# Six plain blocks instead of four at the head of each FFN, in a fused transformer block

## The chip, the cores and the metric

One core of a Trainium2 chip runs the whole kernel. The time is the device time of one execution in microseconds (us). An execution also leaves a profile; its span is the time from the first to the last instruction. TensorE (PE) multiplies, ScalarE (ACT), VectorE (DVE) and GpSimd (POOL) do elementwise work, SyncE (SP) issues nearly all DMAs. Each engine works through its own queue in order.

## The reference

One layer for 512 tokens of width 1024, in fp32: a half-weighted SwiGLU FFN, a mixer with two kinds of attention, and another half-weighted FFN, then a norm.

```
x = x + 0.5 * swiglu(rmsnorm(x, norm_ffn1), w_ffn1_gate, w_ffn1_up, w_ffn1_down)
x = x + hybrid_mixer(rmsnorm(x, norm_mix), w_in, ..., w_out, rel_bias)
x = x + 0.5 * swiglu(rmsnorm(x, norm_ffn2), w_ffn2_gate, w_ffn2_up, w_ffn2_down)
return rmsnorm(x, norm_final)

swiglu(h, w_gate, w_up, w_down) = (silu(h @ w_gate) * (h @ w_up)) @ w_down     # d_ff = 2816
```

The mixer projects x to queries, keys and values of 16 heads of 64. Eight heads do block attention (MoBA; at this length every earlier block of 256 tokens is selected, so it is causal attention with a relative bias), eight do NSA: a compressed branch, a selected branch (all blocks at this length) and a window branch, each weighted by a gate.

## The kernel before

x is held transposed, as eight tiles `xs[k]` of 128 features x 512 tokens. Every fp32 operand of a matmul is split into a high and a low half (`halves`, `split`: ScalarE makes the high half, VectorE the low one, L80/L81 and L196/L197), and a product is three matmuls (`mm3`, L86 to L88): a *triple*. The norm's gain goes into x before the product (`gained`, L122/L123, the 16 `xo` tiles in `ffn.xg`), its per-token root R (a row of 512, `rows_of_roots`) after it.

An FFN has 22 blocks `f` of 128 of d_ff. Its work is a list of `Step`s that `go` puts on TensorE in just that order; loads, sums and splits are given out 26, 12.8 and 8.6 us of step cost ahead. The order on the other engines, and when a buffer is given, is decided by a planner at build time, which simulates the program with its own costs, takes instructions in program order as far as they are ready, and lets a later one go first where an earlier one is not ready or has no buffer.

- `plain(fs)`: blocks without tricks, two halves of the depth (j) and gate and up (m): per block four steps of 12 matmuls of 512 columns. It needs only the gained x. At its end, `finish` scales by R (L260), applies silu, multiplies (L262), and `kept` stores the result `h` as two halves (L224, L225).
- `pair(f)`: two blocks with seven products where plain blocks need eight (Strassen's scheme in Winograd's form): 14 steps of 12 matmuls of 256 columns. It needs sums of weights (L288), weight splits into `sph` and `spl` (three buffers each), and sums and blocks of the normed x: `sums_of_x(k)` (L186 to L190) and `blocks_of_x(k)`, for k from 0 to 3. The first product stays in its bank while a copy `wc` is taken from it (L304).
- `down`: h times the down weights, 8 output tiles times one triple per block; a weight chunk serves eight triples. A finished output tile is added to x (L465).
- `mixed` lays the down triples of the group before between the steps of the pairs of a group.

The FFNs begin with four plain blocks, so that TensorE has work while R and the sums of x are made. Then come 24 (`LEAD`) of the 32 down triples of these blocks unmixed, the other eight beside the next two pairs, and so on in groups of four; the last group has two blocks. FFN1 ends with 16 unmixed triples, FFN2 with 16 in which the roles are turned, so that the result comes out by tokens. `h` tiles come from a pool of 16, which in FFN1 holds seven tiles of the bias tables too. In FFN1 the sums of squares are made from `xs` (`squares`: ScalarE squares, VectorE adds at L138, TensorE sums over partitions at L144).

In the mixer, heads are done in three chunks each of logits, turn and values, with the projections, and later the output product `w_out`, as filler between them: a generator gives out filler units of one depth tile, and `target(i)` says how many of them shall have been given by chunk i (1.4 a chunk in NSA, 0.6 in block attention). `need` forces what a head needs.

```
        def target(i):
            if i < n_nsa:
                return 1.4 * i
            return 1.4 * n_nsa + 0.6 * (i - n_nsa)
```

## Time and profile before

| | |
|---|---|
| time, three runs | median 1039.27 us (1038.64 to 1039.96) |
| the profiled execution | 1037.35 us, span 1035.6 us |
| PE busy | 991.0 us (96%), 6096 matmuls |
| DVE, ACT, POOL busy | 759.1 us (73%), 526.2 us (51%), 138.8 us (13%) |
| mean granted TensorE clock | 0.987 |
| DMA | 104.45 MB, 101 GB/s over the span |

FFN1 reaches from the start to about 370 us, the mixer from there to 672, FFN2 to the end. A page of the profile has the span in 40 slices of 25.9 us; a digit is the busy share of a slice in tenths. A row of the list in order of time reads: start, duration, engine, line, operation, output <- inputs, form, and in brackets how long the engine sat idle before it and who ended that. Matmuls overlap in their pipeline, so the pace is read from their starts and not from their durations.

### The profile page before, as it was taken

To read this page: it belongs to the slowest core of one execution; us is meant where nothing else is said; L and a number is where in the kernel's file an instruction comes from. 1 tells how busy PE (TensorE), PEld (TensorE's weight loads), DVE (VectorE), ACT (ScalarE), POOL (GpSimd) and SP (SyncE) were. 2 spreads that over 40 slices of the span, in tenths; PEclk is the share of its full clock that TensorE was granted. 3 is DMA by queue.
4 is the path that set the end of the run, shared out by engine and by line. 5 is a ranking of instruction groups with operands and counts; after the bars stand their busy time and mean duration, and the time that the engine had idled before them with its cause. 6 is when DMAs were issued, how large, how long until landed. Compare 5 with 4: busy or idle time off the path is not lost.

```text
span 1035.6 us, 15887 instructions
## 1 busy us (share of the span) xinstructions
PE 991.0 (96%) x6096; PEld 868.3 (84%) x6096; DVE 759.1 (73%) x1232; ACT 526.2 (51%) x897; POOL 138.8 (13%) x169
## 2 busy tenths in 40 slices
PE   8979999999999999999999998997999999999996
PEld 6858898999999887787787786686899999999985
DVE  6985758877766486778778966779577776677745
ACT  6633443444443264658667856655244443344326
POOL 0000000000000040046553562500000000000002
PEclk9989999999999999999999999999999999999999
DMA  9323463323321125541011141363333333332102
GB/s 314 120 82 122 123 182 106 122 82 104 121 82 33 52 75 154 177 127 57 30 48 31 52 122 42 102 223 87 97 99 106 97 108 102 123 119 65 62 1 82
DMA packets 40688, 104.45 MB, mean 101 GB/s; under 512 B 9089, under 2 KB 13906, under 8 KB 40612
## 3 DMA queue, kind: packets, MB, share of 16 engines
q1 hardware_dynamic: 40324, 103.29, 32.0%
q8 instruction: 48, 0.79, 0.3%
q14 instruction: 28, 0.23, 0.1%
q10 hardware_dynamic: 288, 0.14, 0.1%
HBM read 97.98 MB, written 5.30 MB: 100 GB/s over the span
## 4 chain that ended last, share of the span: by engine, by line
PE 52%; DVE 5%; ACT 3%; issue 2%; DMA 1%; ACTq 0%; DVEq 0%; SPq 0%
PE pd L87 4%; PE pd L86 4%; PE pd L88 4%; PE pu L86 3%; PE pu L88 3%; PE pu L87 3%; PE pw L87 3%; PE pw L88 3%; PE pw L86 3%; PE pp L88 3%; PE pp L86 3%; PE pp L87 3%; PE ps_t L895 2%; PE pgu L86 1%; PE pgu L87 1%
## 5 line engine op out<-in xcount | busy, mean ns | idle before, releaser
L196 ACT ACTIVATE sph<-aw 128x1024 fp32r<-128x1024 f32 x126 | 133.7, 1061 | 247.7 <-PE pu L87 110.0
L197 DVE TENSOR_TENSOR spl<-aw,sph 128x1024 fp32r<-128x1024 f32 x126 | 153.7, 1221 | 30.6 <-ACT sph L196 30.4
L80 ACT ACTIVATE whi<-raw 128x1024 fp32r<-128x1024 f32 (+3 forms) x109 | 105.7, 971 | 109.3 <-PE pd L87 41.5
L87 PE MATMUL pd<-h,whi 128*128 128x512 f32 x336 | 134.8, 401 | 10.9 <-DVE h L225 10.9
L86 PE MATMUL pd<-h,whi 128*128 128x512 f32 x336 | 134.7, 401 | 3.8 <-DVE x L465 1.8
L88 PE MATMUL pd<-h,wlo 128*128 128x512 f32 x336 | 132.8, 395 | 0.0
L86 PE MATMUL pu<-th,sph 128*128 128x256 f32 x432 | 120.6, 279 | 4.1 <-ACT wc L304 3.3
L88 PE MATMUL pu<-th,spl 128*128 128x256 f32 x432 | 120.1, 278 | 0.0
L87 PE MATMUL pu<-tl,sph 128*128 128x256 f32 x432 | 120.0, 278 | 0.0
L288 DVE TENSOR_TENSOR aw<-aw 128x1024 f32<-128x1024 f32 x72 | 87.8, 1220 | 37.9 <-DMA aw<-in_wgu 37.7
L81 DVE TENSOR_TENSOR wlo<-raw,whi 128x1024 fp32r<-128x1024 f32 (+3 forms) x83 | 100.0, 1207 | 20.0 <-ACT whi L80 19.2
L465 DVE SCALAR_TENSOR_TENSOR x<-pd,x 128x512 f32<-128x512 f32 x88 | 60.3, 688 | 59.1 <-PE pd L88 59.1
L86 PEld LDWEIGHTS pu<-th,sph 128*128 128x128 f32 x432 | 81.1, 188 | 10.1 <-ACT wc L304 5.0
L87 PEld LDWEIGHTS pu<-tl,sph 128*128 128x128 f32 x432 | 81.6, 189 | 3.6
L88 PEld LDWEIGHTS pu<-th,spl 128*128 128x128 f32 x432 | 81.1, 188 | 0.0
L88 PE MATMUL pw<-xo,spl 128*128 128x256 f32 x288 | 79.9, 277 | 0.0
L86 PE MATMUL pw<-xo,sph 128*128 128x256 f32 x288 | 79.9, 277 | 0.0
L87 PE MATMUL pw<-xo,sph 128*128 128x256 f32 x288 | 79.8, 277 | 0.0
L87 PEld LDWEIGHTS pd<-h,whi 128*128 128x128 f32 x336 | 64.3, 191 | 18.3 <-DVE h L225 12.6
L88 PEld LDWEIGHTS pd<-h,wlo 128*128 128x128 f32 x336 | 64.3, 191 | 14.2
L86 PEld LDWEIGHTS pd<-h,whi 128*128 128x128 f32 x336 | 63.9, 190 | 13.5 <-DVE x L465 4.0
L87 PEld LDWEIGHTS pw<-xo,sph 128*128 128x128 f32 x288 | 54.3, 189 | 2.7
(250 smaller groups left out, 2452.9 us busy)
## 6 DMA issues: line engine op xcount, KB each, us to landing
aw<-in_wgu SPq DMA_DIRECT2D x72, 512.0 KB, 4.2
raw<-in_wd1a SPq DMA_DIRECT2D x20, 512.0 KB, 3.5
raw<-in_wd2a SPq DMA_DIRECT2D x20, 512.0 KB, 3.7
raw<-in_w_a SPq DMA_DIRECT2D x16, 512.0 KB, 3.6
raw<-in_wgu SPq DMA_DIRECT2D x15, 512.0 KB, 6.9
raw<-in_w SPq DMA_DIRECT2D x8, 512.0 KB, 5.1
raw<-in_w_o SPq DMA_DIRECT2D x16, 256.0 KB, 3.2
scr_t<-scr_r SPq DMA_DIRECT2D x8, 384.0 KB, 8.6
```

Source lines behind the costliest of these rows:

```text
L80: nc.scalar.activation(hi[:, s], src[:, s], AF.Copy)
L81: (nc.gpsimd if side[0] else nc.vector).tensor_tensor(lo[:, s], src[:, s], f32(hi[:, s]), ALU.subtract)
L86: nc.tensor.matmul(p, w[0], v[0], start=first, stop=False, skip_group_check=again)
L87: nc.tensor.matmul(p, w[0], v[1], start=False, stop=False, skip_group_check=again)
L88: nc.tensor.matmul(p, w[1], v[0], start=False, stop=last, skip_group_check=again)
L196: nc.scalar.activation(hi, v, AF.Copy)
L197: nc.vector.tensor_tensor(lo, v, f32(hi), ALU.subtract)
L288: nc.vector.tensor_tensor(to, x, y, op)
L465: nc.vector.scalar_tensor_tensor(xs[d], p, 0.5, xs[d], ALU.mult, ALU.add)
L895: nc.tensor.transpose(p[:, wide:wide + 128], lps[qi][:, j * 128:(j + 1) * 128], ident)
```

## The change

1. `PLAIN = 6`: both FFNs begin with six plain blocks, in two groups of three (in each group first all j = 0, then all j = 1); 16 blocks are left for eight pairs in four groups of four, and no group of two. Of the 48 triples of the six blocks 12 (`LEAD`) stand unmixed, 36 beside the next two pairs. `sums_of_x` is posted at steps 4, 6, 8, 10 and `blocks_of_x` at 4, 18, 18, 23 (before: sums from step 5 (FFN1) or 4 on, at 0, 1, 3 and 5 steps' distance, blocks at the first, 8, 10, 15). The last group has four blocks: 32 unmixed triples at the end of each FFN.
2. In FFN1 the squares are taken from four token-major tiles of x (128 tokens x 1024), loaded for it, with ScalarE's sum along the row; the additions and TensorE's sum go. The loads stand between the second and the third weight chunk on SP; x4 to x7 come after that. The root is made one step earlier.
3. The softmax of the first two query tiles of a head shares one reciprocal.
4. `target` gives 2.0 units a chunk in block attention.
5. FFN2's last down weights have four blocks; the second half of each goes through the `aw` and `sph`/`spl` buffers.

```diff
+PLAIN = 6
-LEAD = 24
+LEAD = 12
...
+    def begun(ffn, w, posts):
+        steps = [s for f in range(0, PLAIN, 3) for s in ffn.plain(range(f, f + 3))]
+        sums = [(at, lambda k=k: ffn.sums_of_x(k)) for k, at in enumerate((4, 6, 8, 10))]
+        blocks = [(at, lambda k=k: ffn.blocks_of_x(k)) for k, at in enumerate((4, 18, 18, 23))]
+        for at, post in posts + sums + blocks:
+            steps[at].post.append(post)
+        fills = ffn.down(w, range(PLAIN), half_added, "mm", 2)
+        return steps + fills[:LEAD], fills[LEAD:]
...
-        for f in (1, 2):
-            first_w(f, [slice(0, 8)], nc.sync)
-            first_x(2 * f + 2)
-            first_x(2 * f + 3)
+        first_w(1, [slice(0, 8)], nc.sync)
+        tokens = [ffn.raw().rearrange("p a b c -> p (a b c)") for _ in range(NT)]
+        for i in range(NT):
+            nc.sync.dma_start(tokens[i], A["x"][i * 128:(i + 1) * 128])
+        first_w(2, [slice(0, 8)], nc.sync)
+        for k in range(4, NK):
+            first_x(k)
...
-            for k in range(NK):
-                squares(tmp, k, "tmp", 3, nc.vector)
+            for i in range(NT):
+                nc.scalar.activation(tokens[i], tokens[i], AF.Square, accum_out=ss[:, 0, i:i + 1])
...
-        steps = ffn.plain(range(FP), [
-            (0, squares_of_x), (3, lambda: roots(0, sums_of_squares("mm"))), (4, lambda: rows_of_roots(0, "mm")),
-            (8, make_rows), *x_sums(ffn, 5)])
+        steps, fills = begun(ffn, A["wd1"], [
+            (1, squares_of_tokens), (2, lambda: roots(0, ss[:, 0])), (3, lambda: rows_of_roots(0, "mm")),
+            (12, make_rows)])
...
-        for f in range(FP, NF, FP):
-            fs = range(f, min(f + FP, NF))
+        for f in range(PLAIN, NF, FP):
+            fs = range(f, f + FP)
...
-            pairs[62 + 6 * i].post.append(lambda i=i: copied_cmp(i))
+            pairs[54 + 6 * i].post.append(lambda i=i: copied_cmp(i))
...
-                    nc.vector.reciprocal(m[:, 2:3], m[:, 1:2])
+                nc.vector.reciprocal(m[:, :len(qis), 2:3], m[:, :len(qis), 1:2])
...
-            return 1.4 * n_nsa + 0.6 * (i - n_nsa)
+            return 1.4 * n_nsa + 2.0 * (i - n_nsa)
...
-        steps = ffn.plain(range(FP), [
-            (2, lambda: roots(2, sums_of_squares("mm"))), (3, lambda: rows_of_roots(2, "mm")), *x_sums(ffn, 4)])
+        steps, fills = begun(ffn, A["wd2a"], [
+            (2, lambda: roots(2, sums_of_squares("mm"))), (3, lambda: rows_of_roots(2, "mm"))])
...
-        last = range(NF - NF % FP, NF)
-        w = [load(A["wd2b"][half]) for half in range(2)]
+        last = range(NF - FP, NF)
+        w = []
+        for half in range(2):
+            w.append(load(A["wd2b"][half][:, :2]))
+            v = ffn.raw().rearrange("p a b c -> p (a b c)")
+            nc.sync.dma_start(v, A["wd2b"][half][:, 2:].rearrange("p a b -> p (a b)"))
+            hi, lo = [t.rearrange("p a b c -> p (a b c)") for t in ffn.split(v.rearrange("p (a b c) -> p a b c", a=2, b=4))]
+            w[half] += [(hi[:, s], lo[:, s]) for s in (slice(0, S), slice(S, 2 * S))]
```

The down weights are laid out on the host in the new groups.

More of the change, by code (lines that the diff above doesn't have):

```diff
@@ L235, in split, with plain @@
             return hi, lo
-        def plain(self, fs, then_at):
+        def plain(self, fs):
             A, half, bank = {}, {}, {}
@@ L269, in plain @@
                      for j in range(2) for f in fs for m in range(2)]
-            for at, post in then_at:
-                steps[at].post.append(post)
             return steps
@@ L414, in go @@
                     late()
-    def x_sums(ffn, first):
-        return [(at, lambda k=k, part=part: part(k))
-                for k, ats in enumerate(((first, first), (first + 1, 8), (first + 3, 10), (first + 5, 15)))
-                for at, part in zip(ats, (ffn.sums_of_x, ffn.blocks_of_x))]
+    def begun(ffn, w, posts):
[6 more added lines that the diff above has]
+        return steps + fills[:LEAD], fills[LEAD:]
     scr_t = dp.tile([16, 128, RVW], F32, name="scr_t")
@@ L542, in block_kernel @@
             steps += ffn.mixed(own, fills)
-            if len(fs) == FP:
-                fills = ffn.down(A["wd1a"][f // FP], fs, half_added)
+            if fs[-1] < NF - 1:
+                fills = ffn.down(A["wd1"][f:], fs, half_added)
             else:
-                steps += ffn.down(A["wd1b"], fs, then, None, 4)
+                steps += ffn.down(A["wd1"][f:], fs, then, None, 4)
         pairs[18].post.append(put_rows)
@@ L1051, in block_kernel @@
         hs = ffn.hs
-        steps = ffn.plain(range(FP), [
-            (2, lambda: roots(2, sums_of_squares("mm"))), (3, lambda: rows_of_roots(2, "mm")), *x_sums(ffn, 4)])
-        fills = ffn.down(A["wd2a"][0], range(FP), half_added, "mm", 2)
-        steps, fills = steps + fills[:LEAD], fills[LEAD:]
-        for f in range(FP, NF, FP):
-            fs = range(f, min(f + FP, NF))
+        steps, fills = begun(ffn, A["wd2a"], [
+            (2, lambda: roots(2, sums_of_squares("mm"))), (3, lambda: rows_of_roots(2, "mm"))])
+        for f in range(PLAIN, NF, FP):
+            fs = range(f, f + FP)
             steps += ffn.mixed([step for i in fs[::2] for step in ffn.pair(i)], fills)
-            if len(fs) == FP:
-                fills = ffn.down(A["wd2a"][f // FP], fs, half_added)
+            if fs[-1] < NF - 1:
+                fills = ffn.down(A["wd2a"][f:], fs, half_added)
         ffn.go(steps)
@@ L1146, in _down @@
     chunks = []
-    for f in range(0, NF, FP):
-        part = v[:, :, f:f + FP]
-        chunks.append(np.ascontiguousarray(part.reshape(128, -1, 8, 128).transpose(1, 0, 2, 3)))
-    return np.stack(chunks[:-1]), chunks[-1]
+    for f, end in zip((0, *range(PLAIN, NF, FP)), (*range(PLAIN, NF + 1, FP),)):
+        part = v[:, :, f:end]
+        chunks.append(part.reshape(128, -1, 8, 128).transpose(1, 0, 2, 3))
+    return np.ascontiguousarray(np.concatenate(chunks))
 def _laid_out(x, norm_ffn1, w_ffn1_gate, w_ffn1_up, w_ffn1_down, norm_mix, w_in, cmp_pos_k, cmp_w1_k,
@@ L1170, in _laid_out @@
         "wgu1": _gate_up(w_ffn1_gate[0], w_ffn1_up[0]),
-        **dict(zip(("wd1a", "wd1b"), _down(w_ffn1_down[0]))),
+        "x": c(x[0]), "wd1": _down(w_ffn1_down[0]),
         "w_a": _blocks(w_a, D, 128), "w_v": kp(w[:, 1024:1536]), "w_n": kp(w_n),
@@ L1177, in _laid_out @@
         "wgu2": _gate_up(w_ffn2_gate[0], w_ffn2_up[0]),
-        "wd2a": _down(w_ffn2_down[0])[0],
-        "wd2b": _blocks(w_ffn2_down[0][F - F % (FP * 128):], F % (FP * 128), S),
+        "wd2a": _down(w_ffn2_down[0])[:NF - FP],
+        "wd2b": _blocks(w_ffn2_down[0][F - FP * 128:], FP * 128, S),
         "rel_bias": c(rel_bias), "gfin": c(norm_final[None]),
```

18 lines of the change are left out of this document (8 added, 10 removed).

## The prediction

> **What bounds the kernel now.** I read the summary of busy time and the slices first, then the list of waits on TensorE, then the windows around those waits, then the instructions in order of time.
>
> ```profile
> PE 991.0 (96%) x6096; PEld 868.3 (84%) x6096; DVE 759.1 (73%) x1232; ACT 526.2 (51%) x897; POOL 138.8 (13%) x169
> ...
> PE   8979999999999999999999998997999999999996
> ```
>
> TensorE is the bound: 4% of the span isn't busy, and the slices put the holes in few places (at the start, in the third slice, the 25th and the 28th, at the end). So only two things can move the time: the number of matmul columns, and these holes. Who makes them stands in the waits of PE.
>
> ```profile
> engine line waited for: us in total, times, longest us
> PE pd L87 <- DVE h L225: 10.9, 3, 5.1
> PE pu L86 <- ACT wc L304: 3.3, 4, 0.8
> ...
> PE pd L86 <- ACT h L224: 1.6, 2, 0.8
> ...
> PE pgu L87 <- DVE xo L123: 1.4, 3, 0.7
> ```
>
> The longest is the first: the down products of the first plain blocks wait for `h`. In order of time (FFN1's place, then the first pair of FFN2):
>
> ```profile
> 55.74 0.39 PE L86 MATMUL pgu<-xo,whi 128*128 128x512 f32 x1
> ...
> 56.42 0.39 PE L86 MATMUL pd<-h,whi 128*128 128x512 f32 x1
> ...
> 63.69 0.80 PE L87 MATMUL pd<-h,whi 128*128 128x512 f32 x1 [5.11 <-DVE h L225]
> 64.28 0.63 PE L88 MATMUL pd<-h,wlo 128*128 128x512 f32 x1
> 64.71 0.63 PE L86 MATMUL pd<-h,whi 128*128 128x512 f32 x1
> ...
> 742.40 0.28 PE L86 MATMUL pu<-xo,sph 128*128 128x256 f32 x1
> ...
> 745.11 0.28 PE L88 MATMUL pu<-xo,spl 128*128 128x256 f32 x1
> ```
>
> From 55.74 to 56.42 three 512-column matmuls start, 0.227 us each; after the long wait the starts are 0.43 apart (64.28 to 64.71), so the clock is halved for a while. What that costs is in the windows (stretch, length, busy time of PE, PEld, DVE, ACT, POOL, granted clock, DMA share, GB/s); the third and fifth reach from the first down product to the first pair:
>
> ```profile
> 0.00:20.00 20.00, 16.73 (x52) 11.80 (x53) 14.92 (x27) 16.55 (x28) 0.81 (x8) 0.91 0.89 296
> 5.95:68.00 62.05, 53.00 (x219) 41.38 (x219) 57.02 (x96) 39.18 (x63) 0.00 (x0) 0.93 0.55 189
> 56.42:83.78 27.36, 19.87 (x73) 14.58 (x72) 19.46 (x28) 7.50 (x11) 0.00 (x0) 0.88 0.25 77
> 686.00:728.00 42.00, 36.73 (x154) 29.59 (x153) 42.00 (x72) 23.86 (x38) 0.00 (x0) 0.92 0.30 91
> 717.30:742.40 25.10, 19.63 (x75) 14.73 (x74) 16.99 (x25) 7.06 (x9) 0.00 (x0) 0.86 0.29 84
> 628.00:655.00 27.00, 22.00 (x111) 15.70 (x110) 20.27 (x50) 19.07 (x43) 6.67 (x11) 0.97 0.10 30
> ```
>
> The 24 triples (LEAD) are 72 matmuls, 16.3 us. They take 27.4 us in FFN1 and 25.0 in FFN2 (its first began 0.1 after 717.3): 11.0 and 8.7 us lost. Why `h` is late: VectorE is full, 42.0 of 42.0 us in FFN2 from the row of roots R on, 57.0 of 62.05 in FFN1. It has to make the sums and blocks of x, split weights and finish four plain blocks in the 43.5 us (16 steps of 12 x 0.227) that the plain blocks give it, and cannot.
>
> **The change part by part.**
>
> *Two more plain blocks per FFN.* They replace a pair. From 742.40 to 745.11 there are 23 intervals of 256-column matmuls, 0.118 us each. A pair has 7 products x 24 matmuls = 168, 19.8 us; two plain blocks have 96 of 512 columns, 21.8 us. TensorE gets +2.0 us per FFN, **+4.0**, with nothing to hide behind.
>
> *The stall at h.* VectorE's prices in FFN1's first stretch:
>
> ```profile
> L81 DVE TENSOR_TENSOR wlo<-raw,whi 128x1024 fp32r<-128x1024 f32 (+2 forms) x13 | 13.6, 1056 | 2.7 <-ACT whi L80 2.7
> ...
> L260 DVE TENSOR_TENSOR t<-pgu,R 128x512 f32<-128x512 f32 x8 | 5.4, 681 | 0.0
> L138 DVE TENSOR_TENSOR acc<-acc,sq 128x512 f32<-128x512 f32 x7 | 4.8, 687 | 0.1
> L288 DVE TENSOR_TENSOR aw<-aw 128x1024 f32<-128x1024 f32 x3 | 3.7, 1219 | 0.2 <-DMA aw<-in_wgu 0.2
> L197 DVE TENSOR_TENSOR spl<-aw,sph 128x1024 fp32r<-128x1024 f32 x3 | 3.6, 1214 | 0.0
> ```
>
> Each new block adds four 512-column operations (two of L260, the product, the low half): 2.7 us; its two weight chunks are two splits of a full 1024, at the 1.2 us of L288 and L197: 2.4. Two blocks are +10.2, one more down chunk +1.2, and the seven additions of squares go, -4.8: 57.0 becomes 63.6 us. The time given is 24 steps of 2.72 plus 12 triples of 0.68, 73.5 us before the first pair. In FFN2 the 42 us after R become about 53, against 31.3 (686 to 717.3) plus 8 steps of 2.72, 53.1; and 7.3 us of the 53 (L288, L197) are for pairs, not for `h`. The last block's `h` isn't asked for until ten of the 12 triples have run (each group of two columns takes blocks 0 to 4 first), another 6.8 us. So VectorE goes from some 10 us overdrawn to just covered. I leave 1 us at each place, for the queue's order may not be the ideal one: **-10.0** and **-7.7**. Bounds: nothing gained (0), all gone (-19.7). I take the near end because the account closes; what is late next is the blocks of x of the last k (posted at the last plain step, 2 us of work on ScalarE and VectorE), which the 12 triples cover, 8.2 us.
>
> *36 triples beside the first two pairs, before 8.* The four waits of `pu` on `wc` (3.3 us in all) are the copy of u between a pair's third and fourth product; it comes once in each of the four pairs of the two first groups and in none of the 14 others, whose steps have about one triple each between them. The first group gets 36 triples over 28 steps: **-3.3** (bounds 0 and -3.3).
>
> *Squares from token tiles.* Eight squares of 512 columns and seven additions become four ScalarE squares of 1024, the same elements, each into a sum; the sums on TensorE go:
>
> ```profile
> 21.91 0.95 PE L144 MATMUL pr<-ones_f,acc 128*128 128x1 f32 x8
> 22.71 0.49 PE L86 MATMUL pgu<-xo,whi 128*128 128x512 f32 x1
> ```
>
> **-0.8**. The additions no longer stand among the eight gained tiles, for whose low halves TensorE waits 1.4 us at the start (granted clock 0.91 in the first window): **-1.5**, bounds -3 and the price of the DMA. That price: four token tiles of 0.5 MB go ahead of the third weight chunk and x4 to x7 on SP's queue. At the 296 GB/s of the first window, x0-x3, two chunks, the tokens and the third chunk (4.7 MB) land at about 16.7 us, split by 19; TensorE asks for them after two blocks, 5.95+10.9+some 3.5 lost = 20.3. x4 to x7 (5.8 MB) land by 20.2 and are due at 25.8. Covered by 1.3 us; without that cover up to 2.1 MB/296 GB/s = 7.1 us. The four issues on SP cost it 2 us while it has nothing else ready. ScalarE's squares stand ahead of the third chunk's split and the last gained tiles; R comes one step and the sums earlier than now, so VectorE's idle time before R shrinks too (counted in the 1 us left).
>
> *The mixer.* 24 reciprocals fewer out of
>
> ```profile
> L881 DVE RECIPROCAL m<-m 128x1 f32<-128x1 f32 x96 | 13.9, 154 | 7.0 <-ACT lpn L879 3.4 <-ACT lp L879 2.9
> ```
>
> is 3.7 us of an engine that isn't the bound here; what is behind the merged one, the first tile's scaling on POOL, waits for the second exponential, inside a lag of four steps. I give -0.5. The filler: in my count of the generator's units, both rates bring all filler but the last eight output products in before head 6; the new one moves 16 units of w_out from the lump at head 5 to heads 2 to 4. The hole is later, 628 to 655 in the windows above (22.0 busy of 27.0), where no filler is left in either: -0.5, bounds -5 (the hole filled) and +4 (the softmax chains of heads 0 to 4 pushed back by as much again as that hole is worth). **-1.0** together.
>
> *The end.* TensorE's last matmul, and VectorE's residuals of the last two token tiles:
>
> ```profile
> 1026.92 0.39 PE L88 MATMUL pd<-whi,h 128*128 128x512 f32 x1
> ```
>
> ```profile
> 1026.32 0.69 DVE L1081 SCALAR_TENSOR_TENSOR z<-pd,z 128x512 f32<-128x512 f32 x1
> ...
> 1029.05 0.68 DVE L1081 SCALAR_TENSOR_TENSOR z<-pd,z 128x512 f32<-128x512 f32 x1
> ```
>
> The last residual starts 2.1 us after the last matmul did: VectorE needs 2.7 us a tile, as much as the tile's 12 matmuls, and never catches up. With four blocks a tile has 24 matmuls, 5.4 us; VectorE waits for TensorE, and some 0.4 us are left: **-1.7**. The triples themselves only move from the mix to the end.
>
> *Buffers, the cost side.* Twelve `h` tiles of six blocks plus eight of the next two pairs want 20 of 16; by my count tiles free up at triple 41 of 48, step 23 of 28, before block 8 is stored at step 26. In FFN1 seven more hold bias tables until step 18. And at the end two of three `sph`/`spl` slots go to the last down weights, perhaps while the last pair still wants them. **+1.5**, bounds 0 and +9. No cost: layout on the host, the same bytes of down weights, `make_rows` and the `cb` copies at other steps. The `cb` copies still stand on SP's queue ahead of weight loads: 0.
>
> Sum: 4.0 - 10.0 - 7.7 - 3.3 - 0.8 - 1.5 - 1.0 - 1.7 + 1.5 = **-20.5 us**. The profiled execution took 1037.35 (span 1035.6), 1.9 below the median of the three runs: 1016.9 on that scale, **1018.8** on the median's.
>
> **The rivals.**
>
> *Half the stall stays* (VectorE's order puts pair sums and splits before `h`, as it does now): half of 19.7 is 9.9, less the 2.0 already left, +7.9: 1026.7. For it: FFN2's account closes by little. Against: the last `h` has 6.8 us of grace. The Trainium skill ("TensorE: Matmul & The Clock Gate", What's actually happening) says the clock halves only after an idle window of about 3.4 us. The starts 0.43 apart behind the 5.1 us wait agree. By that rule half of the waits (6.3 of the list's 12.5 us, none longer than 2.6) would cost only themselves, less the 2.0: +4.3, 1023.1.
>
> *The start is fed too late*: the third chunk and x4 to x7 behind 2.1 MB of tokens, with ScalarE's queue held by a square whose tile isn't there: +7.1, 1025.9. For: 0.89 of DMA busy in the first 20 us. Against: 1.3 us of cover by the same figure.
>
> *The last pair lacks split slots*: with one slot each product waits for its split, 1.2 us on VectorE and about as much on ScalarE before, less a triple of 0.7: 1.7 at five products, +8.5 less the 1.0 of it counted: 1026.3. For: the loads need only free `aw` tiles, and the last pair needs four of six.
>
> *Better*: the hole at 628 to 655 fills and the head loses little: 1012.
>
> *Nothing gained*: the wait only moves to the first pair (blocks of x late): -20.5+17.7 = 1036.5 to 1039.
>
> *Slower*: the `h` pool. If ScalarE's queue reaches the store of block 8 before the pool has a tile, the splits behind it stop, and TensorE with them, at the end of each FFN's first group. It decides from 11.3 us per FFN (20.5+2.1 over two); a hold of two steps with triples (4.5 us), a refill of two splits (4.5) and the half clock (3) is 12: 1042.8. Against: the count above has the tiles three steps early.
>
> **How the numbers follow.** About 0.2% (2.1 us) is what a measurement can tell from no change. Forecast (1014 to 1023) 0.58; half the stall 0.14; start 0.08; end slots 0.06; better 0.06; nothing gained 0.04; slower 0.04. Low 1012 and high 1029 take in all but the last two and some of their edges. Faster 0.91, same 0.04, slower 0.05.
>
> **What would show it.** Right: no PE wait on `h` L225 above 1 us in either FFN, the 12 triples in 8 to 9 us at full clock; `pu` waits on `wc` gone; no `pr` in FFN1; last residual within 0.5 us of the last matmul; VectorE below 95% in the plain stretch. Wrong: PE waits on `whi` or `xo` in the first 30 us; waits of `pu` on `spl` in the last pair; ScalarE idle before `h` for a tile; a longer hole near heads 5 to 7.

## The result and the profile after

The changed kernel takes 1010.02 us (median of four runs, 1009.3 to 1011.87) against 1038.95 for the kernel before on the same chip: a ratio of 0.9728, with a 95% interval from 0.9705 to 0.975. The forecast was 1018.8, with a range from 1012 to 1029: the direction and the main cause were right, but the time came out 8.8 us lower than forecast and lies 2 us below the range.

From the page of the changed kernel, busy time and slices (its line numbers differ by a few from those of the kernel before: L88 is now L89, L304 is L303):

```profile
PE 983.4 (98%) x5944; PEld 862.0 (86%) x5944; DVE 728.6 (72%) x1171; ACT 516.1 (51%) x883; POOL 141.0 (14%) x169
...
PE   9999999999999999999999999999999999999997
```

The holes in the third and the 28th slice are gone. The one that stood in the 25th is only smaller: its digit is 9 from a busy share of 90% on, and in the worst 27 us TensorE is busy for 23.2 (before 22.0):

```profile
608.00:635.00 27.00, 23.21 (x117) 17.37 (x116) 20.00 (x48) 19.44 (x43) 7.70 (x11) 0.92 0.11 30
```

The waits of TensorE on `h` and on `wc` are gone from the list of waits of the changed kernel, which begins so:

```profile
PE pp L89 <- DVE wlo L82: 2.3, 1, 2.3
PE ps_s L875 <- DVE m L881: 2.1, 10, 0.4
PE pgu L89 <- DVE wlo L82: 1.7, 1, 1.7
...
PE pR L156 <- DVE rc L150: 0.9, 1, 0.9
```

Windows of the changed kernel (columns as in the prediction): the first 20 us; the first down product to the first pair in FFN1 and in FFN2; and the first pair to the last down product of FFN1:

```profile
0.00:20.00 20.00, 18.20 (x71) 14.17 (x72) 8.91 (x16) 14.92 (x24) 0.81 (x8) 1.00 0.89 317
75.92:84.07 8.15, 8.15 (x37) 6.76 (x36) 6.29 (x8) 3.45 (x5) 0.00 (x0) 1.00 0.19 66
720.35:728.51 8.16, 8.16 (x37) 6.76 (x36) 6.31 (x8) 3.46 (x5) 0.00 (x0) 1.00 0.18 65
84.07:353.37 269.30, 269.30 (x1843) 247.19 (x1841) 185.84 (x211) 111.59 (x147) 5.08 (x6) 1.00 0.33 103
```

The 12 triples take 8.15 us, 36 matmuls of 0.227 (8.17), at full clock; nothing is left of the stall. From the starts of the first and last instructions of each kind, the two profiled executions divide like this. "Beyond" means after taking out the moved and added work: 8 plain steps of 2.72 us more per FFN, one pair of 19.74 fewer, 12 triples (8.16) moved from ahead of the pairs to beside and behind them. The work itself is the +4.0.

| stretch | before | after | beyond the moved work | predicted |
|---|---|---|---|---|
| work (two plain blocks for a pair, twice) | | | +4.0 | +4.0 |
| start to first down product | 56.42 | 75.92 | -2.3 | -2.3 |
| first down product to first pair, FFN1 | 27.36 | 8.15 | -11.05 | -10.0 |
| first pair to last down product, FFN1 | 285.62 | 269.30 | -4.7 | -1.65 (`wc`) |
| last down product to first compressed score | 82.22 | 79.72 | -2.5 | 0 |
| first compressed score to first product of FFN2 | 220.08 | 218.91 | -1.2 | -1.0 |
| plain blocks, FFN2 | 45.67 | 68.35 | +0.9 | 0 |
| first down product to first pair, FFN2 | 25.03 | 8.16 | -8.7 | -7.7 |
| first pair to last down product, FFN2 | 284.52 | 272.00 | -0.9 | -1.65 (`wc`) |
| last matmul to the end of the span | 8.68 | 6.99 | -1.7 | -1.7 |
| buffers | | | 0 | +1.5 |
| sum (spans 1035.6 and 1007.5) | | | -28.1 | -20.5 |

The row for the end: the last residual now starts 0.43 us after the last matmul did.

```profile
1000.51 0.40 PE L89 MATMUL pd<-sph,h 128*128 128x512 f32 x1
...
1000.94 0.69 DVE L1084 SCALAR_TENSOR_TENSOR z<-pd,z 128x512 f32<-128x512 f32 x1 [1.14 <-PE pd L89]
```

The sum of the table misses by 7.6 us. The other 1.2 of the 8.8 are the step from the profiled execution to the median: it was 1.9 us in the forecast and is 0.7 (1009.3 to 1010.02) for the changed kernel.

So three things had to be found out: whether the stall was VectorE's amount of work or its order; where the gains came from that no edit names (4.7 and 2.5 us); and whether the small terms that came out right did so for the reason given.

### The profile page after: what moved, and what is told of

Its sections match the earlier page's. It is cut to its first block, busy times and chain, and to the rows that moved or that the text cites. A ratio compares the mean times of both kernels' runs of the same rounds, so it can differ in the third digit from the quotient of the medians.

```text
span 1007.5 us, 15491 instructions
## 1 busy us (share of the span) xinstructions
PE 983.4 (98%) x5944; PEld 862.0 (86%) x5944; DVE 728.6 (72%) x1171; ACT 516.1 (51%) x883; POOL 141.0 (14%) x169
## 4 chain that ended last, share of the span: by engine, by line
PE 89%; DVE 5%; DMA 2%; ACT 2%; issue 1%; SPq 0%; POOL 0%; DVEq 0%; ACTq 0%; POOLq 0%
PE pd L87 8%; PE pd L88 8%; PE pd L89 8%; PE pu L89 6%; PE pu L87 6%; PE pu L88 6%; PE pw L88 4%; PE pw L89 4%; PE pw L87 4%; PE pgu L89 4%; PE pgu L88 4%; PE pgu L87 4%; PE pp L87 3%; PE pp L89 3%; PE pp L88 3%; PE pv L87 2%
## 5 line engine op out<-in xcount | busy, mean ns | idle before, releaser
L197 ACT ACTIVATE sph<-aw 128x1024 fp32r<-128x1024 f32 x114 | 121.0, 1061 | 237.3 <-PE pu L88 118.6
L198 DVE TENSOR_TENSOR spl<-aw,sph 128x1024 fp32r<-128x1024 f32 x114 | 139.2, 1221 | 37.3 <-ACT sph L197 37.1
L88 PE MATMUL pd<-h,whi 128*128 128x512 f32 x320 | 126.4, 395 | 0.0
L87 PE MATMUL pd<-h,whi 128*128 128x512 f32 x320 | 126.1, 394 | 0.0
L89 PE MATMUL pd<-h,wlo 128*128 128x512 f32 x320 | 125.2, 391 | 0.0
L89 PE MATMUL pu<-th,spl 128*128 128x256 f32 x384 | 106.9, 278 | 0.0
L87 PE MATMUL pu<-th,sph 128*128 128x256 f32 x384 | 106.9, 278 | 0.0
L88 PE MATMUL pu<-tl,sph 128*128 128x256 f32 x384 | 106.7, 278 | 0.0
L469 DVE SCALAR_TENSOR_TENSOR x<-pd,x 128x512 f32<-128x512 f32 x72 | 49.3, 688 | 45.8 <-PE pd L89 45.8
L89 PE MATMUL pgu<-xo,wlo 128*128 128x512 f32 x192 | 74.9, 390 | 1.7 <-DVE wlo L82 1.7
L88 PEld LDWEIGHTS pu<-tl,sph 128*128 128x128 f32 x384 | 72.6, 189 | 4.0
L88 PE MATMUL pgu<-xo,whi 128*128 128x512 f32 x192 | 74.9, 390 | 0.3 <-DVE xo L124 0.3
L87 PE MATMUL pgu<-xo,whi 128*128 128x512 f32 x192 | 75.1, 391 | 0.0
L89 PEld LDWEIGHTS pu<-th,spl 128*128 128x128 f32 x384 | 72.1, 188 | 0.0
L89 PEld LDWEIGHTS pd<-h,wlo 128*128 128x128 f32 x320 | 60.1, 188 | 13.4
L89 PE MATMUL pw<-xo,spl 128*128 128x256 f32 x256 | 70.9, 277 | 0.0
L87 PE MATMUL pw<-xo,sph 128*128 128x256 f32 x256 | 70.8, 276 | 0.0
L88 PE MATMUL pw<-xo,sph 128*128 128x256 f32 x256 | 70.8, 276 | 0.0
```

What stands on the lines that cost most here:

```text
L87: nc.tensor.matmul(p, w[0], v[0], start=first, stop=False, skip_group_check=again)
L88: nc.tensor.matmul(p, w[0], v[1], start=False, stop=False, skip_group_check=again)
L89: nc.tensor.matmul(p, w[1], v[0], start=False, stop=last, skip_group_check=again)
L197: nc.scalar.activation(hi, v, AF.Copy)
L198: nc.vector.tensor_tensor(lo, v, f32(hi), ALU.subtract)
L469: nc.vector.scalar_tensor_tensor(xs[d], p, 0.5, xs[d], ALU.mult, ALU.add)
```

## The experiments

Two theories on the stall at `h`. *Amount*: between the row of roots and `h` VectorE has more work than TensorE gives it time. *Order*: it has time, but pairs' work stands ahead of `h`. Times are given beside the kernel before on the same chip, as a ratio with its 95% interval.

### Four low halves on GpSimd (e1)

```diff
-            (nc.gpsimd if side[0] else nc.vector).tensor_tensor(lo[:, s], ...)
+            (nc.gpsimd if side[0] or pool else nc.vector).tensor_tensor(lo[:, s], ...)
...
-  half[f, j] = halves(A.pop((f, j)), ...)
+  half[f, j] = halves(A.pop((f, j)), ..., j == 1)
```

The text below names the halves of `h`; what the edit moves are the low halves of the second weight chunk of each plain block, 1024 columns, 1.2 us on VectorE.

> The kernel before, with the low halves of the four plain blocks' h written by GpSimd instead of VectorE: four operations of about 1.2 us less for VectorE in each FFN's plain stretch, nothing else moved. Theory (VectorE is overdrawn by the work itself): the stall at h, 11.0 us in FFN1 and 8.7 in FFN2, shrinks by about 5 us at each place, since the clock's half-rate tail goes with it; time some 8 to 10 us below the kernel before. Rival (the order of VectorE's queue, pairs' work ahead of h, makes the stall whatever the amount): the stall stays above 8 and 6 us, and the time falls by less than 4 us.

1046.05 us, ratio 1.0063 (1.0045 to 1.0081): slower. The stalls stay (27.05 us to the first pair in FFN1, 27.36 before; 28.5 in FFN2, 25.0 before). In the order of time of FFN2:

```profile
690.01 2.38 POOL L81 TENSOR_TENSOR wlo<-raw,whi 128x1024 fp32r<-128x1024 f32 x1 [7.53 <-ACT whi L80]
697.87 11.04 POOL L81 TENSOR_TENSOR wlo<-raw,whi 128x1024 fp32r<-128x1024 f32 x2 [5.48 <-DVE xo L197]
...
703.75 2.91 DVE L186 SCALAR_TENSOR_TENSOR xa<-x,gcol,R 128x512 f32<-128x512 f32 x1
706.58 2.88 DVE L197 TENSOR_TENSOR tl<-xb,th 128x512 fp32r<-128x512 f32 x1
```

The first of these halves took GpSimd 2.4 us, while VectorE was busy for 0.5 us of it. The two of the second row took 8.2 and 2.8 us, with VectorE busy throughout, and the VectorE operation that ran at the end of each took 2.9 us instead of 0.7. The relief was eaten on the spot, so this run decides nothing between the theories; e9 does it without GpSimd.

### The second low halves left out (e9)

```diff
-            (nc.gpsimd if side[0] else nc.vector).tensor_tensor(lo[:, s], ...)
+            if low:                       # not for j == 1; lo is hi there
+                (nc.gpsimd if side[0] else nc.vector).tensor_tensor(lo[:, s], ...)
```

> The kernel before without the low halves of the second weight chunk of each plain block (TensorE multiplies by the high halves once more in their place, so its work is the same): VectorE has four operations of 1.2 us less in each plain stretch, behind the row of roots, and GpSimd has nothing to do with it. Theory (the amount of VectorE's work between the roots and h sets the stall): the stalls, 10.9 us in FFN1 and 8.7 in FFN2, fall by 4 to 6 us each, time 8 to 12 us below the kernel before. Rival (the planner's order, pairs' work ahead of h, sets it whatever the amount): each falls by less than 2, time within 4 us.

1031.42 us, ratio 0.9917 (0.9895 to 0.9939). The first down product to the first pair takes 24.07 us instead of 27.36 in FFN1, the same stretch in FFN2 3.6 less. Waits on `h` in the list fall from 10.9 us to this:

```profile
PE pd L89 <- DVE h L227: 4.6, 4, 2.9
```

Less than the 4 to 6 expected, but 3.3 and 3.6 us of stall for 4.8 us of work: the amount counts, at some 0.7 for 1. The spread of these stretches in executions of the same instructions (e6 and e7 below) is smaller: 27.3 to 28.1 us in FFN1, 24.5 to 25.4 in FFN2.

### VectorE ordered by hand (e10)

```diff
-            with tc.manual_schedule(engines={mybir.EngineType.PE}):
+            with tc.manual_schedule(engines={mybir.EngineType.PE, mybir.EngineType.DVE}):
...
+        # blocks of x for k = 1, 2, 3 posted behind triples 7, 13 and 19
+        [steps[16 + 6 * k].post.append(lambda k=k: ffn.blocks_of_x(k)) for k in (1, 2, 3)]
```

> The kernel before with VectorE's order in the two FFNs written out in the order of the program instead of by the planner, and the last three blocks of x posted on the triples, behind h. The amount of work is the same. Theory (amount): what is gained at h is lost at the waits of the first pair or of the triples; from the first down product to the first pair still 6 to 11 us are lost. Rival (order): with h first, 16.3 us of triples take less than 20 in both FFNs, 7 us or more gained at each. The rest of the FFNs, ordered by hand too, may lose time, so the stretches count and not the whole.

1045.17 us, ratio 1.0055 (1.0038 to 1.0072). With `h` ahead of the blocks of x the triples take 21.7 us in FFN1 (27.4 before) and 22.9 in FFN2 (25.0), so 5.4 and 6.6 are still lost, though the waits on `h` themselves fall from 10.9 us to 0.5; and the plain blocks before them wait for their weight splits instead, 9.2 us more in FFN1, 4.4 in FFN2:

```profile
58.26 0.80 PE L88 MATMUL pgu<-xo,wlo 128*128 128x512 f32 x1 [5.70 <-DVE wlo L81]
...
PE pd L87 <- DVE h L225: 0.5, 2, 0.2
```

From the first product to the first pair FFN1 takes 81.4 us (77.8 before), FFN2 73.0 (70.7). This order moves the loss and does not remove it. It is no proof that none could: in this run VectorE stood idle for 9.1 of the 37.8 us between the roots and the first down product of FFN1, and for 7.6 of 36.5 in FFN2, where the kernel before had no idle time. And counted to the first pair and not to `h`, VectorE of the kernel before is overdrawn by little: it did 48.6 us of work from the roots to the first pair of FFN1 and 48.8 in FFN2, and without a stall there would have been 45.5 and 48.2 us for it (29.2 and 31.9 to the first down product, and the 16.3 of the 24 triples). So less work there shortens the stall (e9), but an order that puts `h` in time and keeps VectorE busy might have saved part of it too; no run tried one.

### Blocks of x posted later (e6)

```diff
-  ((first, first), (first + 1, 8), (first + 3, 10), (first + 5, 15))
+  ((first, first), (first + 1, 15), (first + 3, 15), (first + 5, 15))
```

> The kernel before with the last three blocks of x posted at the last plain step (15) in both FFNs instead of at steps 8, 10 and 15: VectorE's work is the same, only its order changes, h first. Theory (amount): the waits on h shrink, and the pairs' first products, or the triples, wait for the blocks instead; TensorE loses about the same from the first down product to the second pair, time within 3 us of the kernel before. Rival (order): the loss falls by half or more in both FFNs, time 8 to 12 us below.

1039.5 us, ratio 1.0011 (0.9996 to 1.0025). The run tells neither: all instructions come in the same order as before, on every engine. The planner places the blocks by its own costs, wherever they are posted. The posting steps 4, 18, 18, 23 of the change do nothing either: built with 4, 8, 10, 15, the changed kernel has the same instructions in the same order. What the run is good for is the noise: it is the kernel before once more, and so is e7 below.

### Token squares in the kernel before (e5)

```diff
-        for f in (1, 2): first_w(f, ...); first_x(2 * f + 2); first_x(2 * f + 3)
+        first_w(1, ...); four token tiles; first_w(2, ...); first_x(4) ... first_x(7)
...
-            (0, squares_of_x), (3, lambda: roots(0, sums_of_squares("mm"))), (4, ...rows),
+            (1, squares_of_tokens), (2, lambda: roots(0, ss[:, 0])), (3, ...rows),
```

> The kernel before with the changed kernel's beginning alone: token tiles loaded ahead of the third weight chunk, their squares on ScalarE, no additions on VectorE and no sums on TensorE in FFN1; four plain blocks and all else as before. VectorE loses seven additions, 4.8 us. Theory (VectorE's amount of work sets the stall at h): FFN1's stall, 11.0 us, falls by 4 to 7; with the 2.3 us of the start, 6 to 9 us below the kernel before, FFN2 unchanged. Rival (the order sets it): the start gains 2.3 us, the stall stays above 9; 2 to 4 us below the kernel before.

1038.8 us, ratio 0.9999 (0.9987 to 1.0012): neither came. VectorE's first operation behind the row of roots, in this kernel and in the kernel before:

```profile
22.27 0.75 DVE L186 SCALAR_TENSOR_TENSOR xa<-x,gcol,R 128x512 f32<-128x512 f32 x1 [0.33 <-ACT R L157]
```

```profile
27.30 0.75 DVE L186 SCALAR_TENSOR_TENSOR xa<-x,gcol,R 128x512 f32<-128x512 f32 x1 [1.59 <-ACT R L157]
```

The roots come 5 us earlier, and the sums of x with them; but they now stand ahead of the split of the fourth weight chunk, for which TensorE waits:

```profile
28.94 0.50 PE L88 MATMUL pgu<-xo,wlo 128*128 128x512 f32 x1 [2.70 <-DVE wlo L81]
```

The stretch to the first down product is not shorter (50.9 us from the first product, 50.5 before) and the stall only 0.8 shorter. The additions that went had been done before the roots, in time that VectorE could not use for `h` anyway.

### The beginning undone, and the plain blocks alone (e13, e12)

e13 is the reverse of the diff of e5, in the changed kernel. e12 undoes that and the two edits of the mixer as well (below, e8), so that six plain blocks, 12 triples and the end are what is left.

> The changed kernel with its beginning alone as before. Theory (with the token squares the sums on TensorE go, but TensorE waits for the fourth weight chunk instead, so the net is about nothing): from the first product to the first down product within 1 us of the changed kernel's 69.4, and no wait for a weight chunk at 27 us. Rival (the beginning is worth its predicted 2.3 us): that stretch 2 to 3 us longer.

> The changed kernel with its beginning (squares, their sums, the order of the first loads) and its mixer as before: what is left of the change are the six plain blocks, the 12 triples and the end. Theory (these are the whole gain): time within 1.5 us of the changed kernel, the 12 triples of each FFN in 8.2 us, no wait on h. Rival (the beginning and the mixer carry their predicted 3.3 us, and VectorE's 4.8 us of additions come back as a stall in FFN1): 3 to 9 us above the changed kernel.

e13: 1012.38 us, ratio 0.9745 (0.9717 to 0.9772). e12: 1013.97, ratio 0.9764 (0.974 to 0.9788), so 24 of the 29 us are those of the plain blocks, the 12 triples and the end. Against the changed kernel's ratio of 0.9728 e13 is 1.8 us and e12 3.7 us slower; by its expectation e12 is with its rival (3 to 9), although no stall came back, but the intervals of all three overlap. Neither waits for `h`, and the triples take 8.15 and 8.16 us. The two have the same beginning, and yet from the first product to the first down product e13 needs 72.7 us, e12 69.8 (the changed kernel 69.4). The first 20 us of e12, and of e13:

```profile
0.00:20.00 20.00, 16.98 (x60) 12.67 (x61) 15.10 (x27) 15.25 (x25) 0.81 (x8) 1.00 0.87 297
```

```profile
0.00:20.00 20.00, 16.22 (x48) 11.54 (x49) 14.21 (x27) 14.98 (x25) 0.81 (x8) 0.91 0.84 282
```

So e13's profile, 3.3 us longer than the changed kernel's, is with its rival too (2 to 3). But with the same beginning the granted clock was 0.91 in one execution and 1.00 in the other. Of the 2.8 us between them 1.8 are the clock (0.09 of 20 us), 0.7 longer waits for gained tiles. The 2.3 us that the beginning seemed to gain lie within that. At a clock of 1.00, five profiles with token squares and the rows of roots at the same step in FFN1 (the changed kernel, e4, e8, e16, e17) need 69.4 to 70.1 us from the first product to the first down product, e12 with the old beginning 69.8. Over all profiles, the eleven with the old loads and squares had 0.91 here in five, the nine with token squares in none: it may be that the denser start spares TensorE the slow phase, which would be worth about 1 us in the mean, but these are few.

### The mixer undone (e8)

```diff
-                nc.vector.reciprocal(m[:, :len(qis), 2:3], m[:, :len(qis), 1:2])
+                    nc.vector.reciprocal(m[:, j, 2:3], m[:, j, 1:2])      # for each query tile
...
-            return 1.4 * n_nsa + 2.0 * (i - n_nsa)
+            return 1.4 * n_nsa + 0.6 * (i - n_nsa)
```

> The changed kernel with the mixer as before: a reciprocal for each query tile of 128, and 0.6 units of filler for each step of block attention. Theory (the mixer's two edits are worth about 1 us): first block score to first product of FFN2 1.0 to 1.3 us longer, time 0.5 to 2 us above the changed kernel. Rival (they are worth nothing, or cost): time the same as the changed kernel or below it.

1010.79 us, ratio 0.973 (0.971 to 0.9749), and the stretch took 218.5 us: the same as the changed kernel. One profile cannot tell here. All of them together do: seven profiles with both edits (without e17) have 217.0 to 219.3, mean 218.5; twelve without 218.5 to 221.6, mean 219.9. The difference is 1.5 us, with some 0.8 of uncertainty; ten of the twelve have four plain blocks, so it is not the two edits alone that divide them.

### Low halves twice (e3)

```diff
+            if twice:
+                nc.vector.tensor_tensor(lo[:, s], src[:, s], f32(hi[:, s]), ALU.subtract)
```

These are again the halves of the weight chunks, 11 in each FFN (the text names `h`).

> The changed kernel, with the low half of each plain block's h computed twice on VectorE (the second writes the same values): about 11 operations of 1.2 us more in each FFN's plain stretch, 13 us. Theory (six plain blocks leave VectorE a margin of about 10 us in FFN1 and 9 in FFN2): the wait on h comes back with 3 to 5 us at each place and a half-rate tail of 2 to 3, time 8 to 14 us above the changed kernel. Rival (VectorE's amount of work was not what held h, the new order was): no wait on h over 1 us, time within 2 us of the changed kernel.

1017.94 us, ratio 0.9788 (0.9754 to 0.9823): 7.9 us above the changed kernel (6.2 by the ratios), but not at `h`. FFN2 behind the roots, and the one large wait, in FFN1:

```profile
672.00:727.84 55.84, 54.49 (x240) 44.73 (x240) 55.48 (x85) 27.66 (x43) 0.00 (x0) 1.00 0.30 97
```

```profile
31.23 0.80 PE L91 MATMUL pgu<-xo,wlo 128*128 128x512 f32 x1 [5.75 <-DVE wlo L84]
```

VectorE is full (in the changed kernel 47.0 us of 54.1), and still `h` is in time, against the expectation. But only eight of the eleven operations, 9.7 us, stand between the roots and the last `h` in FFN2; the others came ahead of the roots, where VectorE had time. So what was added just fills the margin of 9 us and does not overdraw it: the run can't bring the stall back, and does not decide between amount and order. In FFN1 the early chunks are late, which costs 6.6 us and gives VectorE the time back.

### 40 triples ahead (e4)

```diff
-LEAD = 12
+LEAD = 40
```

> The changed kernel with 40 triples ahead of the first pair instead of 12, so 8 are left beside the first two pairs, as before. Theory (a pair without triples beside it waits for its copy of u): four waits of pu on wc, 0.8 us each, come back, 3.3 us; time 2.5 to 3.5 us above the changed kernel. Rival (those waits went with the relief of VectorE and ScalarE, not with the triples): no wc waits, time within 0.7 us.

1017.63 us, ratio 0.9803 (0.9754 to 0.9853).

```profile
PE pu L87 <- ACT wc L303: 3.3, 4, 0.8
...
PE pd L87 <- DVE x L469: 2.1, 3, 1.7
```

The four waits come back as expected, and each costs 0.99 us by the starts around it, 4.0 in all. The rest of the 7.6 was not expected. The lump of 40 triples takes 28.5 us in each FFN, 1.3 more than its work. And in FFN1 two waits stand between the pairs that the changed kernel does not have, 1.69 us for a residual and, 1.7 us later, 0.77 for a sum, while VectorE has waited 10.6 us for a load of weights:

```profile
178.18 0.50 PE L87 MATMUL pd<-h,whi 128*128 128x512 f32 x1 [1.69 <-DVE x L469]
...
175.16 1.23 DVE L287 TENSOR_TENSOR aw<-aw 128x1024 f32<-128x1024 f32 x1 [10.63 <-DMA aw<-in_wgu]
```

The kernel before has the same pair of waits at 158 us, which is what the next four runs are about.

### The waits at 158 us (e2, e7, e11, e18)

In the kernel before, TensorE waited twice between FFN1's pairs, while VectorE waited 10.7 us for a load of weights:

```profile
158.27 0.50 PE L86 MATMUL pd<-h,whi 128*128 128x512 f32 x1 [1.75 <-DVE x L465]
160.00 0.39 PE L86 MATMUL pu<-th,sph 128*128 128x256 f32 x1 [0.77 <-DVE t L319]
```

```profile
155.25 1.22 DVE L288 TENSOR_TENSOR aw<-aw 128x1024 f32<-128x1024 f32 x1 [10.70 <-DMA aw<-in_wgu]
```

From 119 to 150 us SyncE's queue was issuing the eight big bias writes and 32 small copies. e2 moves the copies to ScalarE's queue, e7 posts them 18 pair steps later, e11 spreads the big writes, e18 makes the tables themselves later and with them all of it.

```diff
e2:  -                nc.sync.dma_start(cb[...]      +                nc.scalar.dma_start(cb[...]
e7:  -            pairs[62 + 6 * i]                  +            pairs[80 + 6 * i]
e11: -            pairs[26 + 3 * i]                  +            pairs[26 + 9 * i]
e18: -            pairs[18].post.append(put_rows)    +            pairs[46].post.append(put_rows)
e18: -            pairs[26 + 3 * i]                  +            pairs[50 + 3 * i]
```

> The kernel before, with the 32 copies of the compressed bias issued from ScalarE's DMA queue instead of SyncE's. Theory (SyncE's queue, busy with the bias copies, posts a pair's weights late): TensorE's waits at 155 to 160 us (about 2.5 us with their tail) go, time 2 to 3 us below the kernel before, if the issues cost ScalarE nothing. Rival (the DMA engines themselves are what is late, or the wait has another cause): the waits stay, no change beyond 1 us.

> The kernel before with the copies of the compressed bias begun 18 pair steps (about 35 us) later. Theory (these copies stand on SyncE's queue ahead of two weight loads of a pair): TensorE's waits near 155 to 160 us, 2.5 us and some tail, go, and time falls by 2 to 3 us unless the copies hit other loads. Rival (the eight big bias writes, which stay where they were, hold the loads): the waits stay, time within 1 us of the kernel before.

> The kernel before with the eight big bias writes of 384 KB set nine pair steps apart instead of three, the small copies where they were; the order on all engines but the DMA queue's stays. Theory (the big writes, back to back on SyncE's queue, hold two weight loads of a pair): TensorE's waits near 155 to 160 us (2 to 4 us with tails in the runs of the kernel before) go, time 2 to 3 us below. Rival (the small copies hold them, or the loads are late for another cause): the waits stay, time within 1 us.

> The kernel before with the bias tables made 28 pair steps (some 50 us) later, so that all their writes and copies, which e7 left where they were, come later on SyncE's queue; TensorE's and VectorE's work is otherwise the same. Theory (these transfers hold the weight loads of a pair): no wait of TensorE between 140 and 165 us, and the stretch from the first pair to the last down product of FFN1 falls from the 285.6 to 288.5 us of three executions to 282.9, unless the transfers hit another pair some 50 us later, where a like wait then stands. Rival (the waits belong to the order of that pair's loads and sums): they stay at 155 to 160 us, and the stretch stays above 285.

e2: 1037.81 us, ratio 0.9985 (0.9966 to 1.0005); the waits move to 140 and 143 us (0.64 and 1.74), where ScalarE's splits are now late: its queue stood 3 to 5 us at a time behind the issues.

e7: 1038.74, ratio 0.999 (0.9975 to 1.0004). It tells nothing of the copies: the planner issues them as soon as their source is there, at 129 to 152 us as before, and all instructions come in the same order. It shows how far the waits vary in one program: they were 1.75 and 0.77 us in the kernel before, in e6 1.14 and 0.77, and here

```profile
160.07 0.50 PE L86 MATMUL pd<-h,whi 128*128 128x512 f32 x1 [3.03 <-DVE x L465]
161.80 0.38 PE L86 MATMUL pu<-th,sph 128*128 128x256 f32 x1 [0.77 <-DVE t L319]
```

e11: 1037.78, ratio 0.9988 (0.9978 to 0.9998). The first wait is 0.33 us, below that spread, the second 0.75.

e18: 1033.28, ratio 0.9939 (0.9924 to 0.9954). TensorE waits for nothing but `wc` in the whole stretch from the first pair to the last down product, which takes 282.6 us instead of 285.6 to 288.5, as the theory has it (282.9). VectorE's long wait for weights is

```profile
210.68 1.23 DVE L288 TENSOR_TENSOR aw<-aw 128x1024 f32<-128x1024 f32 x1 [5.88 <-DMA aw<-in_wgu]
```

now, and TensorE does not feel it. So the bias transfers hold the weights, and whether TensorE pays depends on which pair they meet. In the changed kernel the tables come at 138.9 us instead of 115.4, and again no wait follows: in the stretch the changed kernel and six variants with 12 triples ahead have 269.29 or 269.30, e17 has 269.6 and e14 270.1 (with a wait of 0.52 us for a sum at 178 us). The two more plain blocks alone do not bring this about: e4 has them too, its tables come at 135.4 us, and both waits stand there. It takes the 36 triples beside the first two pairs. Whether these help because the transfers meet another pair, or because each pair gives its loads more time, no run separates. The whole time of e18 fell by more, 6.7 us, than the 3 to 6 us of this stretch; where the rest comes from is open.

### The row of roots later (e14, e15, e16)

```diff
FFN1 e14: -(3, lambda: rows_of_roots(0, "mm"))      +(4, ...)
FFN1 e15: -(2, ...roots), (3, ...rows), sums at 4   +(3, ...roots), (5, ...rows), sums at 5
FFN2 e14, e15, e16: -(3, lambda: rows_of_roots(2, "mm"))   +(4, ...)
```

> The changed kernel with the row of roots posted one plain step later in both FFNs (steps 4 and 4 instead of 3 and 3); on VectorE the split of the fourth weight chunk then comes ahead of the sums of x. Theory (the sums of x, made ready early by the early roots, hold the split): the 1.7 us wait at 27 us goes, and the 0.95 us wait for the reciprocal in FFN2; 1.5 to 2.7 us below the changed kernel. Rival (the chunk itself is late, or VectorE's margin is used up): the wait stays, or a wait on h takes its place; time the same or above.

> As the kernel with the row of roots at step 4, but at step 5 in FFN1, with the roots themselves a step later too. Theory (VectorE's margin of some 9 us covers the 2.7 us that the sums of x begin later): the same time as with step 4. Rival (the margin is less): a wait on h or on a block of x comes back, 1 us or more above it.

> The changed kernel with the row of roots one plain step later in FFN2 alone. Theory (the reciprocal of the roots comes 1 to 2 us too late for step 3 there, and VectorE's margin covers the later start): the wait of 0.95 us goes, FFN2's plain stretch 66.9 instead of 68.1 us as in e14 and e15, time 1.0 to 1.5 us below the changed kernel. Rival (a wait on h takes its place, or the beginning of the stretch pays): the stretch stays at 68 or more, time the same.

e14: 1010.38 us, ratio 0.9732 (0.9711 to 0.9753). e15: 1010.47, ratio 0.9731 (0.9709 to 0.9754). The wait of the changed kernel at 27 us (1.7, in its list of waits) goes and comes back eleven microseconds later, at a later chunk (e14; e15 has it at 39.4 us):

```profile
38.84 0.76 PE L89 MATMUL pgu<-xo,wlo 128*128 128x512 f32 x1 [2.01 <-DVE wlo L82]
```

So the early roots alone are not to blame: when they come later, another split is late. In FFN2 both behave as expected, 66.9 us from the first to the last matmul of the plain blocks instead of 68.1 (the table's 68.35 reach to the first down product). e16 has that alone: 1009.79 us, ratio 0.9721 (0.9696 to 0.9745); the stretch is 66.9 us, and the 1.2 us are too little to show in the whole time.

### The positions on GpSimd (e17)

```diff
                             nc.vector.tensor_tensor(          # e16, and this on nc.gpsimd
                                 xv[half(l), 8 * e:8 * e + 8, g, 0:31], tv[half(g), l:16:2, e:e + 31],
```

> The same, with the additions of the positions to the keys and values (two groups of eight 64x248 operations) on GpSimd instead of VectorE, where 4.3 us of them stand ahead of the split for which TensorE waits 2.35 us behind FFN1. Theory (that queue makes the wait): the wait goes, from the last down product of FFN1 to the first compressed score 2 to 3 us less, time 3 to 4 us below the changed kernel. Rival (the additions take GpSimd as long as they held VectorE, and what is computed from them is late instead, or VectorE is slowed beside GpSimd as in e1): the gain of that stretch is under 0.7, or another wait takes its place.

1006.67 us, ratio 0.9695 (0.967 to 0.9721): the fastest median of all, 3.1 us below e16's, though the two intervals overlap. The 20 us behind FFN1, of the changed kernel and of this one, and GpSimd's row:

```profile
372.00:392.00 20.00, 17.65 (x95) 14.96 (x94) 15.05 (x23) 11.25 (x20) 0.15 (x1) 1.00 0.58 158
```

```profile
372.00:392.00 20.00, 20.00 (x106) 16.97 (x106) 13.20 (x17) 12.01 (x21) 6.95 (x8) 1.00 0.62 161
```

```profile
371.16 7.81 POOL L697 TENSOR_TENSOR raw<-t,pos 64x248 f32<-64x248 f32 x8 [9.40 <-DVE t L591]
```

TensorE has no hole there any more. GpSimd needs 7.8 us for what took VectorE 4.3, but nothing waits for it at once. A wait of `pv` for a high half of ScalarE (1.7 us, at 410 us) takes part of the place, so from the last down product to the first compressed score 1.6 us are gained against the changed kernel's own profile, and 3.2 against that of e16, which had a clock of 0.79 behind its wait.

## Why the prediction had the mechanism right and the time 8.8 us too high

**Right.** What bounded the kernel and what the change buys: VectorE was late with `h`, less work behind the roots makes it less late (e9), and two more plain blocks give it the time (e12: no wait on `h` is left). That the amount alone made the stall is not shown: counted to the first pair, VectorE was overdrawn by 3.1 and 0.6 us, not by the prediction's "some 10" (worked out under e10). The account of FFN2 was 53 us of work; the changed kernel has 47.0 and 6.3 in its two windows, 53.3. The end (-1.7) and the `wc` waits (e4) came as worked out, the waits at 4.0 us, tails and all, instead of 3.3. The +4.0 of the plain blocks stands in the table as it was worked out; by the starts the 168 matmuls of the pair that went took 19.3 us between the other pairs and not 19.74, so the work is nearer to +4.8. That also explains the stretch of FFN2, where only 0.9 us show: by the starts, 2.1 us of waits go, but 0.4 are lost on the price of the pair, 0.3 on the 12 triples (8.4 us here instead of 8.16) and 0.45 on the 32 matmuls of 128x128 near the end, which take 3.7 us instead of 3.2. Of the rivals, half a stall, a head starved of loads, a last pair without split slots and a store without an `h` tile show in no wait of the changed kernel.

**The step that failed most: "I leave 1 us at each place".** Nothing was left: -11.05 and -8.7 for -10.0 and -7.7. And "+1.5" for the buffers was nothing. These 3.5 us were allowances for which no row of the trace stood. The account itself closed, with 6.8 us of grace for the last `h`; in FFN2 of the changed kernel VectorE was idle for 7.1 of the 54.1 us behind the roots, and in e3 another 9.7 us went in there without a wait on `h`.

**"The `cb` copies still stand on SP's queue ahead of weight loads: 0."** The step looked at the copies and asked whether the change makes them worse. The waits already there, 1.75 and 0.77 us in the quoted execution, with their tails 2.7 of that stretch's 4.7, were taken for fixed. They go when the tables come later (e18), and in the changed kernel they go with the 36 triples beside the first pairs and come back without them (e4). So the term for these triples, -3.3 with a bound of -3.3, was too small: it counted the `wc` waits alone. The step on the copies asked what stands ahead of the weight loads and not how long TensorE pays for that now. This is the largest term that the sum did not have and that the change itself brings.

**The transition, 0 predicted, 2.5 measured.** The wait behind FFN1 stayed (2.15 us before, 2.35 after). What differs is the clock behind it, and that is chance. The window of 8 us behind this wait, in the kernel before, in e6 and e7 (the same instructions), and in the changed kernel:

```profile
392.73:400.73 8.00, 8.00 (x33) 6.64 (x34) 4.84 (x11) 4.21 (x8) 0.00 (x0) 0.79 0.61 197
```

```profile
395.39:403.39 8.00, 8.00 (x33) 6.63 (x34) 4.82 (x11) 4.20 (x8) 0.00 (x0) 0.79 0.60 197
```

```profile
396.20:404.20 8.00, 8.00 (x43) 6.94 (x44) 6.43 (x13) 5.76 (x10) 0.00 (x0) 1.00 0.62 197
```

```profile
376.34:384.34 8.00, 8.00 (x43) 6.97 (x44) 6.45 (x13) 6.18 (x11) 0.00 (x0) 1.00 0.63 195
```

33 matmuls in 8 us at 0.79, 43 at full clock: some 1.7 us (0.21 of 8). In eighteen profiles with this wait, six had it: four of nine with four plain blocks and two of nine with six. So of the 2.5 us about 1.7 belong to the one profile and not to the change.

**Right for the wrong reason: the beginning, -2.3.** e5 gives 0, and e12 and e13, with one and the same beginning, differ by 2.8. The price, a split that comes behind the sums of x (1.7 us in the changed kernel, 2.7 in e5, 2.0 at a later chunk in e14), was not in the working, which looked at the third chunk and the loads. The 4.8 us of additions counted as relief for FFN1's `h` were none (e5: 0.8).

**The range.** Its low end, 1012, was built from one mechanism, the hole in the mixer. The two allowances that might not be needed (3.5 us) and the waits of the profile before that could go (1.75 and 0.77 near 158 us, 2.15 behind FFN1) would have put it at 1010.6, and at 1008.9 with the 1.7 us of the clock.

## What to carry to other kernels

When an engine off the critical path makes the stall, count its work between the event that releases it and each deadline, not over the whole stretch, and then trust the account: an allowance needs a row of the trace as much as a gain does. A move to another engine gained where nothing waited for the result at once (e17) and lost where the two engines were both busy (e1). And a wait in the profile before that no edit names is a term with a range, not a constant; so is the clock's state behind each wait.

## What was not expected of the hardware

The clock behind one and the same wait is not the same from execution to execution: 0.79 or 1.00 after a wait of TensorE of 2.15 us, and in the first 20 us 0.91 or 1.00. The kernel before, e6 and e7 have the same instructions and show three of the combinations: 0.91 and 0.79, 1.00 and 0.79, 0.91 and 1.00. The prediction weighed the rule of the Trainium skill ("TensorE: Matmul & The Clock Gate", What's actually happening) that only an idle window of about 3.4 us halves the clock; here 2.15 us were enough in four executions out of nine, and 2.35 to 2.38 us in two of six with six plain blocks, so by these runs the length of the wait alone does not decide.

Beside a busy VectorE, GpSimd took 8.2 and 2.8 us for subtractions of 128x1024 that otherwise took it 2.4, and single VectorE operations of 0.7 us took 2.9 at their ends (e1).
